# In-projection of the first mixer: more unused products, an earlier turn, a longer list of loads; in the heads, the later tile of a pair first

## The chip, the cores and the metric

The kernel runs on one core of one Trainium2 chip. The metric is device time in microseconds, the median of the runs shown. A core has TensorE (PE in the profile; its weight loads are PEld), VectorE (DVE), ScalarE (ACT), GpSimd (POOL) and SyncE (SP), whose queue issues nearly all DMAs here. The engines run on their own and meet through semaphores.

## The reference, cut to what matters

One inference step of a two-layer diffusion backbone, for 128 context tokens and 128 latent tokens, which the kernel handles side by side as 256 columns:

```
mod = silu(cond) @ w_ada[l] + b_ada[l]            # six vectors a layer: shift, scale, gate, twice
h = rmsnorm(x, g_norm_mix[l]) * (1 + sc1) + sh1
# layer 0: proj = h @ w_in; 8 MLA heads + 8 GQA heads; out projection
# layer 1: differential attention, 8 heads
x = x + gt1 * mixer(h)
h = rmsnorm(x, g_norm_ffn[l]) * (1 + sc2) + sh2
x = x + gt2 * conv_ffn(h)                          # gated, width-3 convolution over positions
```

All the data are fp32. D_MODEL is 2048, D_FF 5632. The weights are read once: 609 MB.

## The kernel before, in words

**Split products.** A weight tile `raw` (one megabyte, three buffers) is split by ScalarE into a rounded part `wh` and by VectorE into the rest `wl` (`split`, lines 257 to 259); the activations are split in the same way. One product of a 128x128 block is then three fast matmuls of 256 columns: wh by high, wh by low, wl by high (`gemm`, line 366). A plain fp32 matmul, as the unused ones are, takes two passes on TensorE.

**The modulation vectors.** `mod` is needed before the layer can be modulated, so units of w_ada (4 megabytes each, four tiles t = 0 to 3) are computed beside the products, in three ways. `HalfUnit` does half a unit for the very first rows. `sum_rows` multiplies a tile by the condition on TensorE (four matmuls of two passes a tile, which use a quarter of the array's columns each), over the four tiles of a unit into one bank; then ScalarE copies the sums to `am`, TensorE turns them (4 transposes), and VectorE reduces them into `mod` (`ada_finish`, whose steps are `copy` and `turn`). `Deep` does units on VectorE, in two halves of the rows, after a Silu of the condition's half (`silu`, line 527), in the wide tile `condb`.

**The in-projection (`mixer_ab`).** It has 23 output chunks of 128 rows and is swept in parts over the 16 blocks of input rows (a block, or row for short, is 128 of the 2048 features): `whole` takes rows 0 and 1, `halves` 2 and 3, then come three quarters of four rows each with the weights `rest`. A chunk takes 6 matmuls in the first two parts and 12 in the quarters. The results of a part are copied to or added to `proj`, `kvb` and `qb` (L1182, L1184). `part` does for each chunk: `lead` (split weights ahead until n + 8 blocks are ready; only in the first four parts), the product, the copy or add, then what `between` hangs on that chunk. In a quarter, `quarter(q)` hangs on the chunks the sums of two units in pairs of tiles, the turn of each unit, and after the second turn the four modulated rows for the next quarter (`rows`, `modulate`; ScalarE L691 and L692, VectorE L688 and L674). A tile of `rest` holds 16 blocks, the last of a quarter 12; a chunk uses 4.

**What sets the order.** `keep_order` pins instructions to program order on their engine; up to the end of the second quarter TensorE is wholly pinned (`pe.in_turn`), as are the splits of `lead`, the rows and the loads of `Feed`. What isn't pinned is placed by the framework's planner from its own estimate of when operands are ready. `Feed` holds a written list of loads, each with a home (a buffer); a load is issued in that order once its home is free, and `use` frees a home at the point of the program where its last reader stands. Of `rest`'s 18 tiles 13 are in the list; the other five are loaded by `take` when their chunk comes up. In the third quarter (`finish`) nothing of this is pinned; attention's preparations are started there chunk by chunk, `caches()` has loaded the cached keys and split the cached latent `ckc` into `kv_in`, and `Deep` begins.

**The start.** `WARM` unused products of zeros (am, 128x512, fp32) run while the first loads are on their way. Then come the sums of the first half units, the mean square of x, the first two rows, and the projection at 25.41 us.

**The heads.** For each pair of heads there are the query products (`qn`, `qr`), the keys (`kn`, copied by ScalarE at L1355), the values, scores and softmax. `pump` after a product advances the attention's chains, `Deep`, and by `row_step` the units of `ROWS`: tiles 0 and 1 are loaded as a pair (two `araw` buffers), `sum_pair` sums them 8 quarter steps later, then come 2 and 3. The sums are pinned among themselves; between them the planner may place other products.

Of the kernel before, what the change touches and what calls it, by code (L numbers as in the profile page):

```python
# [18 lines left out]
P = 128  # L19
D = 2048  # L20
KD = D // P
T = 128
# [27 lines left out]
    _n += _w  # L50
NCONST = _n
NEARLY = _AT["bada"][0] + 2 * KD
WARM = 9
RATE = {"in0": 0.35, "in": 0.5, "in3": 0.25, "heads": 0.72, "out0": 0.62, "c": 0.36, "outc": 0.36}
FRATE = {"up": 0.7, "down": 1.42}
PEW = {"heads": 1.0, "out0": 1.0, "c": 1.0}
# [38 lines left out]
def step_kernel(ctx: ExitStack, tc: tile.TileContext, A: dict):  # L95
    nc = tc.nc
    dve, act, pool, sp = nc.vector, nc.scalar, nc.gpsimd, nc.sync
    kept = []

    def keep_order(i):  # L100
        if not any(i is j for j in kept):
            kept[:] = [i]
            tc.keep_in_program_order(i)
# [16 lines left out]
    pe = TensorE()  # L120
# [20 lines left out]
    def T_(pl, shape, tag, dt=F32, bufs=None):  # L141
        kw = {} if bufs is None else {"bufs": bufs}
        return pl.tile(shape, dt, tag=tag, name=nm(tag), **kw)
# [44 lines left out]
    def start(g):  # L188
        if next(g, chains) is not chains:
            chains.append(g)  # L190
# [66 lines left out]
    def split(out_hi, out_lo, src, pin=lambda i: i):  # L257
        pin(act.copy(out_hi, src))  # L258
        pin(dve.tensor_tensor(out=out_lo, in0=src, in1=out_hi.bitcast(F32), op=ALU.subtract))  # L259
# [231 lines left out]
            feat["i"] += 1  # L491
            feat["t"] = 0

    def sum_rows(t, raw, ps=None):
        if t == 0:
            ada["ps"] = ps or T_(ppool["ada"], [P, 512], "ada", bufs=1)
        for g in range(4):
            i = pe.matmul(ada["ps"][32 * g:32 * g + 32, :], condw[:, 4 * t + g, :], raw[:, g],
                          start=(t == 0), stop=(t == 3), skip_group_check=True)
            if pinned[0]:  # L500
                keep_order(i)


    class Deep:

        def __init__(self):
            self.steps, self.due, self.rate = [], 0.0, 0.0
            self.loads, self.got, self.mid, self.ahead = [], [], False, False

        def begin(self, home, units, tiles, part, junk):  # L510
            self.home, self.tiles, self.part, self.junk, self.rate = home, tiles, part, junk, 0.0
# [14 lines left out]

        def silu(self):
            keep_order(act.activation(self.row, self.row, AF.Silu))

        def sums(self, half, i, u, t, c):  # L530
            if c == 0:
# [68 lines left out]
    def row_step(until=len(ROWS)):  # L600
        if later:
            later.pop(0)()
        if ada["i"] >= until:
            return
        l, j, q = ROWS[ada["i"]]
        t, g = divmod(ada["t"], 4)

        def load(t):
            ada["raw"] = T_(wpool, [P, 4, 512], "araw", bufs=2)
            sp.dma_start(out=ada["raw"], in_=A["w_ada"][l, j, q, t])  # L610
            return ada["raw"]

        def sum_pair(t, pair):
            for i in range(2):
                sum_rows(t + i, pair[i])

        if pinned[0]:
            if (t, g) == (2, 0):
                sum_pair(0, ada["pair"])
            if t % 2 == 0 and g < 2:  # L620
                ada["pair"] = [load(t)] if g == 0 else ada["pair"] + [load(t + 1)]
            if (t, g) == (3, 3):
                last = ada["pair"]
                later.append(lambda: sum_pair(2, last))
        else:
            if g == 0:
                load(t)
            if g == 3:
                sum_rows(t, ada["raw"])
        ada["t"] += 1  # L630
        if ada["t"] == 16:
            later.extend(ada_finish(l, j, q))
            ada["i"] += 1
            ada["t"] = 0
# [318 lines left out]
    def mixer_ab(hx, beside):  # L953
        l = 0
        with tc.tile_pool(name="ab", bufs=1) as ab:
            with tc.tile_pool(name="abp", bufs=1) as pj:
# [6 lines left out]

                def caches():
                    keep_order(sp.dma_start(out=ckc, in_=A["cache_ckv"]))
                    split(kv_in[:, :, 0, T:2 * T], kv_in[:, :, 1, T:2 * T], ckc)
                    keep_order(sp.dma_start(out=kr[:, T:2 * T], in_=A["cache_krope"]))
                    keep_order(sp.dma_start(out=kg[:, :, T:2 * T], in_=A["cache_gqa_k"]))
                    keep_order(sp.dma_start(out=vg[:, 1], in_=A["cache_gqa_v"]))
# [35 lines left out]
                def half_sums(unit):  # L1005
                    pair_sums(("half", unit.j, unit.h), unit.sums)
# [10 lines left out]
                def weights(w, parts=1):  # L1017
                    feed.add("raw", lambda: w.begin(parts))
# [20 lines left out]
                for q in (1, 2):  # L1039
                    for u, t in ((2 * q + 2, 0), (2 * q + 2, 2), (2 * q + 3, 0), (2 * q + 3, 2)):  # L1040
                        weights(rest)
                        units(u, t)
                        if (q, u, t) == (1, 4, 2):
                            feed.add("late", late_constants)
                    weights(rest)
                    weights(rest)
                feed.go()

                pe.in_turn = True
# [20 lines left out]
                nts = scaled_rows(rb0, 0, 2)  # L1070
                unit = HalfUnit(0, 0, att_bank, att_bank)
                half_sums(unit)

                def first_rows():
                    unit.copy()
                    unit.turn()
                    for c in range(2):
                        begin_row(hx, nts[c], c)

# [71 lines left out]
                    yield  # L1151

                def finish(c):
                    if c == 7:
                        deep.silu()
                        deep.rate = SIDE["in3"]
                    if c < 6:
                        start(queries(c))
                    elif c < 10:
                        start(latents(c - 6))  # L1160
                    elif c == 10:
                        start(key_rope())
                    elif c < 13:
                        start(keys(c - 11))
                    elif c == 14:
                        start(values(0))
                    elif c == 15:
                        start(values(1))
# [22 lines left out]
                def normed(q):  # L1191
                    second["nt"] = []
                    for c in range(4 * q, 4 * q + 4):
                        h = T_(tmp, [P, NT], "nt", bufs=4)
                        keep_order(dve.tensor_tensor(out=h, in0=x[:, c], in1=rb0, op=ALU.mult))
                        second["nt"].append(h)
# [20 lines left out]
                def pair(u, t):  # L1217
                    unit_pair(ROWS[u], t)
                    if t == 2:
                        second["finish"] = ada_finish(*ROWS[u])  # L1220
                        second["finish"].pop(0)()

                def turned(q=0):
                    second["finish"].pop(0)()
                    if q:
                        rows(q)
# [14 lines left out]
                def quarter(q):  # L1241
                    u = 2 * q + 2
                    return {3: lambda: pair(u, 0), 6: lambda: pair(u, 2), 8: turned, 11: lambda: pair(u + 1, 0),
                            12: lambda: normed(q + 1), 14: lambda: pair(u + 1, 2), 16: lambda: turned(q + 1)}

                def at(steps):
                    return lambda c: steps[c]() if c in steps else None
# [15 lines left out]
            with tc.tile_pool(name="abh", bufs=1) as hp:  # L1263
# [61 lines left out]
                weigh_lambda()  # L1325
                accs[:] = [0, 1]
                start(gqa_query(0))
                deep.tiles.append((ab, "kvb"))
                deep.junk = o[:, 6:8]
                deep.rate, deep.ahead = SIDE["heads"], True  # L1330
                for h in range(0, 8, 2):
                    for i in range(2):
                        ps = gemm(WQ.chunk(), qh, qlo)
                        qn[h + i] = T_(hp, [P, NT], "qn", bufs=4)
                        act.copy(qn[h + i], ps)
                        pump(RATE["heads"])
                    ps = gemm(WQ.chunk(), qh, qlo)
                    if h == 6:
                        deep.junk = ql[:, 0:2]
                    ev = T_(tmp, [P, NT], "nt", bufs=4)  # L1340
                    act.copy(ev, ps)
                    qr = T_(hp, [P, NT], "qr", bufs=2)
                    act.copy(qr[:, 0:T], ev[:, 0:T])
                    rope(qr[:, None, T:], ev[:, None, T:], 1, 32, "rcm", "rsm")
                    pump(RATE["heads"])
                    if h == 6:
                        deep.settle()
                    kn = []
                    for i in range(2):
                        if h + i < 7:  # L1350
                            start(gqa_query(h + i + 1))
                        start(gqa(h + i))
                        ps = gemm(WK.chunk(), kh, klo, 3 * T)
                        kn.append(T_(hp, [P, 3 * T], "kn", bufs=2))
                        act.copy(kn[i], ps)  # L1355
                        pump(RATE["heads"])
                    mla_pair(h, qr, kn, values())
                flush()
# [478 lines left out]
```

## Time and profile before

| | |
|---|---|
| median of 3 runs | 2295.28 us (2294.23 to 2295.8) |
| profiled execution | 2295.23 us, span 2293.4 us |
| TensorE busy | 2272.2 us, 99% |
| VectorE, ScalarE, GpSimd busy | 1880.7, 1215.1, 190.9 us |
| mean granted clock of TensorE | 0.996 |
| loads of w_in_ab, 18 of 1 MB | 9.0 us to landing (median) |
| loads of w_ada by TensorE's tile araw, 132 of 1 MB | 6.2 us to landing (median) |

A row of the timeline reads: start, length, engine, line, operation, tiles written and read, shapes, count, and in brackets the idle time of the engine before it with what ended it. A matmul's end is modelled, so busy TensorE is not TensorE at its peak; the spacing of starts says more. The granted clock is the share of full speed that TensorE's clock gate passed.

### The profile page before, as it was taken

The numbers are of one execution on the slowest core, as the hardware profiler recorded it, in microseconds if no ns is written. First come the engines' busy times: TensorE is split into PE (matmuls) and PEld (weight loads), VectorE is DVE, ScalarE is ACT, GpSimd is POOL, SyncE is SP. The second block draws the span as 40 slices with busy tenths as digits, with TensorE's granted clock in tenths as the row PEclk, the third lists the DMA queues.
The fourth block names the chain that finished last, engine by engine and source line by source line (L and its number), as shares of the span: only waits on it lengthen the run. The fifth ranks groups of instructions, "written<-read, shape, count | busy, mean of one in ns | idle before, by whom it ended". The sixth has DMA issues, their size and how long they took to land.

```text
span 2293.4 us, 47509 instructions
## 1 busy us (share of the span) xinstructions
PE 2272.2 (99%) x19496; PEld 2180.4 (95%) x19496; DVE 1880.7 (82%) x2963; ACT 1215.1 (53%) x2049; POOL 190.9 (8%) x219
## 2 busy tenths in 40 slices
PE   9999999999999999999999999999999999999998
PEld 6788888999999999999999999999999999999998
DVE  4768878889989999999978988898899955666654
ACT  4446666765553355555575454557555434555543
POOL 0011104400000000001130000023000000000011
PEclk9999999999999999999999999999999999999999
DMA  9888988777778777777778888776677655555553
GB/s 394 363 354 307 333 329 349 288 264 255 260 259 296 293 274 258 257 268 257 286 292 301 324 316 308 264 273 224 255 260 258 256 201 196 191 198 189 200 188 127
DMA packets 100121, 617.14 MB, mean 269 GB/s; under 512 B 10752, under 2 KB 18880, under 8 KB 33344
## 3 DMA queue, kind: packets, MB, share of 16 engines
q1 hardware_dynamic: 99904, 614.11, 72.4%
q8 instruction: 153, 2.51, 0.4%
q14 instruction: 64, 0.52, 0.1%
HBM read 609.32 MB, written 4.75 MB: 268 GB/s over the span
## 4 chain that ended last, share of the span: by engine, by line
PE 96%; DVE 1%; DMA 1%; ACT 1%; POOL 1%; issue 0%; SPq 0%; DVEq 0%; ACTq 0%
PE acc L110 89%; PE ada L110 3%; PE att L110 2%; DMA raw<-w_in_ab 1%; PE misc L110 0%; DVE wl L259 0%; DMA araw<-w_ada 0%; PE att L113 0%; POOL dev L837 0%; PE ada L113 0%; PE misc L113 0%; ACT wh L258 0%; DVE x L1694 0%; POOL hxc L841 0%; DVE qb L1184 0%
## 5 line engine op out<-in xcount | busy, mean ns | idle before, releaser
L110 PE MATMUL acc<-hx,wh 128*128 128x256 f32 (+1 forms) x7232 | 1248.5, 278 | 3.7 <-ACT wh L258 1.5
L258 ACT CAST wh<-raw 128x1024 fp32r<-128x1024 f32 (+1 forms) x866 | 798.6, 938 | 825.5 <-PE acc L110 697.2
L259 DVE TENSOR_TENSOR wl<-raw,wh 128x1024 fp32r<-128x1024 f32 (+1 forms) x866 | 930.3, 1091 | 245.6 <-ACT wh L258 237.9
L110 PEld LDWEIGHTS acc<-hx,wh 128*128 128x128 f32 x7232 | 1092.8, 188 | 24.7 <-issue 14.2
L110 PE MATMUL acc<-hx,wl 128*128 128x256 f32 (+1 forms) x3616 | 1001.5, 277 | 0.8 <-DVE wl L259 0.7
L110 PEld LDWEIGHTS acc<-hx,wl 128*128 128x128 f32 x3616 | 680.0, 188 | 4.3 <-issue 1.7
L110 PE MATMUL acc<-g,wh 128*128 128x256 f32 x2816 | 478.8, 276 | 0.0
L110 PEld LDWEIGHTS acc<-g,wh 128*128 128x128 f32 x2816 | 423.9, 188 | 0.0
L110 PE MATMUL acc<-g,wl 128*128 128x256 f32 x1408 | 388.0, 276 | 0.0
L483 DVE CUSTOM_DVE_ANT_0 junk<-araw,condb 128x2048 f32<-128x2048 f32 x128 | 294.1, 2297 | 0.0
L110 PEld LDWEIGHTS acc<-g,wl 128*128 128x128 f32 x1408 | 264.2, 188 | 0.0
L211 POOL TENSOR_TENSOR sqacc<-sqacc,sq 128x256 f32<-128x256 f32 x62 | 72.2, 1165 | 1442.3 <-ACT sq L207 1437.6
L110 PE MATMUL acc<-hxc,wh 128*128 128x256 f32 (+1 forms) x1056 | 189.1, 281 | 0.0
L110 PEld LDWEIGHTS acc<-hxc,wh 128*128 128x128 f32 x1056 | 161.9, 188 | 1.8 <-issue 1.7
L110 PE MATMUL acc<-hxc,wl 128*128 128x256 f32 (+1 forms) x528 | 146.8, 278 | 0.0
L110 PEld LDWEIGHTS acc<-hxc,wl 128*128 128x128 f32 x528 | 99.5, 188 | 0.2
L110 PE MATMUL acc<-wh,hxc 128*128 128x256 f32 (+1 forms) x512 | 95.0, 283 | 0.8 <-DVE nt L848 0.8
L1587 ACT ACTIVATE cv<-acc,convw 128x256 f32<-128x256 f32 x169 | 94.4, 559 | 0.0
L538 DVE CUSTOM_DVE_ANT_0 hx<-block,condb 128x1024 fp32r<-128x1024 f32 x66 | 80.4, 1218 | 4.7 <-DMA block<-w_ada 4.4
L1593 DVE SCALAR_TENSOR_TENSOR cv<-acc,convw,cv 128x254 f32<-128x254 f32 x169 | 80.8, 478 | 3.2
L110 PEld LDWEIGHTS acc<-wh,hxc 128*128 128x128 f32 x512 | 79.4, 188 | 3.7 <-issue 2.5
L1590 DVE SCALAR_TENSOR_TENSOR cv<-acc,convw,cv 128x254 f32<-128x254 f32 x169 | 80.2, 474 | 0.0
(290 smaller groups left out, 1809.3 us busy)
## 6 DMA issues: line engine op xcount, KB each, us to landing
raw<-w_up SPq DMA_DIRECT2D x176, 1024.0 KB, 4.8
araw<-w_ada SPq DMA_DIRECT2D x132, 1024.0 KB, 6.2
raw<-w_down SPq DMA_DIRECT2D x88, 1024.0 KB, 4.8
raw<-w_in_c SPq DMA_DIRECT2D x48, 1024.0 KB, 6.9
block<-w_ada SPq DMA_DIRECT2D x42, 512.0 KB, 6.5
raw<-w_in_ab SPq DMA_DIRECT2D x18, 1024.0 KB, 9.0
raw<-w_out_ab SPq DMA_DIRECT2D x16, 1024.0 KB, 7.8
raw<-w_out_c SPq DMA_DIRECT2D x16, 1024.0 KB, 5.6
```

The lines of the kernel that those rows point to most:

```text
L110: return self.placed(nc.tensor.matmul(*a, **kw))
L211: eng.tensor_tensor(out=st["acc"], in0=st["acc"], in1=sq, op=ALU.add)
L258: pin(act.copy(out_hi, src))
L259: pin(dve.tensor_tensor(out=out_lo, in0=src, in1=out_hi.bitcast(F32), op=ALU.subtract))
L483: keep_order(dve.tensor_tensor_reduce(out=T_(feat["pool"], [P, D], "junk"), in1=feat["row"][:, c], in0=feat["raw"].rearrange("p g n -> p ( ...
L538: keep_order(dve.tensor_tensor_reduce(out=self.junk, in0=self.raw, in1=self.row[:, c].rearrange("p (g n) -> p g n", g=2), scale=1.0, scala ...
L1587: pin(act.activation(y, ps, AF.Identity, scale=cw[:, 1, m:m + 1], bias=cw[:, 3, m:m + 1]))
L1590: pin(dve.scalar_tensor_tensor(out=y3[:, :, 1:], in0=p3[:, :, :T - 1], scalar=cw[:, 0, m:m + 1], in1=y3[:, :, 1:], op0=ALU.mult, op1=ALU.add))
L1593: pin(dve.scalar_tensor_tensor(out=y3[:, :, :T - 1], in0=p3[:, :, 1:], scalar=cw[:, 2, m:m + 1], in1=y3[:, :, :T - 1], op0=ALU.mult, op1=A ...
```

## The change

Seven edits, all in what runs before the first feed-forward layer's first products:

1. `WARM` goes from 9 to 15 unused products.
2. `idle_products(2)` twice: two unused fp32 products of x by x (128x512), once after the sums of the second half unit and once after its turn. They write a bank that nobody reads.
3. In the quarters, the second unit's turn and the rows of the next quarter hang on chunk 15, not 16.
4. The other five tiles of `rest` enter the list of `Feed`.
5. The split of the cached latent leaves `caches()` and hangs on chunk 3 of the third quarter.
6. `sum_pair` sums tile 1 before tile 0, and tile 3 before tile 2; start and stop flags go with that order.
7. After a Silu of `Deep` in the heads the next two copies of `kn` go to VectorE.

```
-WARM = 9
+WARM = 15
...
-    def sum_rows(t, raw, ps=None):
-        if t == 0:
-            ada["ps"] = ps or T_(ppool["ada"], [P, 512], "ada", bufs=1)
+    def sum_rows(t, raw, order=(0, 1, 2, 3)):
+        if t == order[0]:
+            ada["ps"] = T_(ppool["ada"], [P, 512], "ada", bufs=1)
         for g in range(4):
             i = pe.matmul(ada["ps"][32 * g:32 * g + 32, :], condw[:, 4 * t + g, :], raw[:, g],
-                          start=(t == 0), stop=(t == 3), skip_group_check=True)
+                          start=(t == order[0]), stop=(t == order[3]), skip_group_check=True)
...
+            self.copies = []
...
         def silu(self):
             keep_order(act.activation(self.row, self.row, AF.Silu))
+            self.copies = [dve.tensor_copy] * 2
+
+        def copy(self):
+            return self.copies.pop() if self.copies else act.copy
...
         def sum_pair(t, pair):
-            for i in range(2):
-                sum_rows(t + i, pair[i])
+            for i in (1, 0):
+                sum_rows(t + i, pair[i], (1, 0, 3, 2))
...
                 def caches():
                     keep_order(sp.dma_start(out=ckc, in_=A["cache_ckv"]))
-                    split(kv_in[:, :, 0, T:2 * T], kv_in[:, :, 1, T:2 * T], ckc)
...
                     weights(rest)
+                    weights(rest)
+                for _ in range(5):
                     weights(rest)
                 feed.go()
...
                 half_sums(unit)
+                unused = acc_bank()
+
+                def idle_products(n):
+                    for _ in range(n):
+                        pe.matmul(unused, x[:, 0, :P], x[:, 0:2].rearrange("p c n -> p (c n)"), start=True, stop=True)
+
+                idle_products(2)
 
                 def first_rows():
                     unit.copy()
                     unit.turn()
+                    idle_products(2)
...
                 def finish(c):
+                    if c == 3:
+                        split(kv_in[:, :, 0, T:2 * T], kv_in[:, :, 1, T:2 * T], ckc)
...
-                            12: lambda: normed(q + 1), 14: lambda: pair(u + 1, 2), 16: lambda: turned(q + 1)}
+                            12: lambda: normed(q + 1), 14: lambda: pair(u + 1, 2), 15: lambda: turned(q + 1)}
...
                 start(gqa_query(0))
+                deep.copies = []
...
-                        act.copy(kn[i], ps)
+                        deep.copy()(kn[i], ps)
```

## The prediction

> **What bounds the kernel now.** I read the page first, then busy time by stage, then the list of TensorE's waits, and only then the timeline of the places that the change touches.
>
> ```profile
> PE 2272.2 (99%) x19496; PEld 2180.4 (95%) x19496; DVE 1880.7 (82%) x2963; ACT 1215.1 (53%) x2049; POOL 190.9 (8%) x219
> ```
>
> ```profile
> 0.00:80.00 80.00, 74.03 (x564) 54.56 (x565) 45.02 (x116) 38.22 (x86) 1.41 (x6) 0.94 0.98 395
> 80.00:160.00 80.00, 78.07 (x656) 64.72 (x655) 51.23 (x118) 30.80 (x62) 3.34 (x4) 1.00 0.91 366
> 160.00:330.00 170.00, 168.83 (x1280) 138.57 (x1279) 140.85 (x340) 111.19 (x264) 23.28 (x27) 1.00 0.85 311
> 460.00:1155.00 695.00, 695.00 (x6133) 695.00 (x6132) 644.44 (x839) 355.95 (x494) 17.54 (x14) 1.00 0.73 269
> ```
>
> The second fence is the table of stages: length, then busy time of PE, weight load, VectorE, ScalarE, GpSimd, then granted clock, DMA share, GB/s. TensorE bounds almost all of it: 695 busy of 695 us in the first feed-forward layer. Everything edited lies before about 365 us. There PE is idle 6.0 us in the first 80, 1.9 in the next 80, 1.2 in the heads. Idle PE, a low clock and PE's own instructions are all that can be won there, a few microseconds in all; what the edits can add is of the same size.
>
> ```profile
> PE acc L110 <- ACT wh L258: 1.5, 3, 0.8
> PE acc L110 <- ACT kn L1355: 0.8, 1, 0.8
> PE acc L110 <- DVE wl L259: 0.7, 2, 0.3
> ```
>
> This is the list of PE's waits from 80 to 460 us (total, times, longest): split weights (wh, wl) that come late, and one late copy of kn. The change aims at these.
>
> **Start: six more products on zeros, four more on x.**
>
> ```profile
> 1.44 9.81 PE L110 MATMUL acc<-am 128*128 128x512 f32 x18 [1.44 <-DVE am L1651]
> ...
> 13.39 1.07 PE L110 MATMUL ada<-araw,condw 128*32 128x256 f32 x16 [2.14 <-DMA araw<-w_ada]
> ...
> 22.17 1.06 PE L110 MATMUL att<-kv_in,condw 128*32 128x256 f32 x16
> 23.79 0.44 PE L113 MATMUL att<-cst,am 128*128 128x128 f32 x2 [0.56 <-ACT am L413]
> 25.41 0.97 PE L110 MATMUL acc<-hx,wh 128*128 128x256 f32 x2 [1.19 <-ACT hx L715]
> ```
>
> ```profile
> 9.80 0.19 PEld L110 LDWEIGHTS acc<-am 128*128 128x128 f32 x1 [0.24 <-issue]
> ```
>
> ```profile
> 15.40:22.20 6.80, 6.80 (x51) 4.26 (x54) 1.69 (x8) 0.54 (x2) 0.70 (x1) 0.50 1.02 420
> 22.30:25.60 3.30, 1.55 (x23) 0.64 (x15) 1.94 (x8) 1.66 (x6) 0.00 (x0) 1.00 1.02 419
> 25.70:29.00 3.30, 3.30 (x16) 3.20 (x16) 2.53 (x6) 2.43 (x6) 0.00 (x0) 0.50 1.00 418
> ```
>
> Nine products are 18 passes, 0.43 us each at full clock (a weight load of 0.19 and 0.24 to the next), so 0.86 a product. Six more take 5.2 us: the stream ends at 16.4, not 11.25, and the first useful sums wait until then, 3.0 us later than 13.39, though their tile is there. In return the clock, which was at 0.50 from 15.4 to 22.2, may stay full: of the 9.8 us between 13.39 and 23.2 some 6.8 ran at half rate, so at full rate they need 6.4, and the sums end at 22.8; with one stretch of 3.4 us still at half, at 24.5. Before it was 23.2. Then two unused products (1.7), the turn (0.44), two more (1.7): the projection starts 3.85 us on, at 26.7 to 28.4, at full clock. Before it started at 25.41 but ran at 0.50 until 29.0, as good as a full-rate start at 27.2. So PE stands between 0.5 us ahead and 1.2 behind.
>
> Sentences on the notes: the Trainium skill (TensorE: Matmul & The Clock Gate, Part 1: The HAM clock gate) says that the gate closes after a whole idle window of about 3.4 us, and its practical advice is only to avoid idle gaps above some 3 us. By that rule gaps as short as those before 25.41 would close nothing, the new products there would be pure cost, and this term would come out about 1.5 us dearer, the whole at 2297.2. The trace differs: after gaps of 0.56 and 1.19 us in a stretch busy 1.55 of 3.30 us the clock stood at 0.50, so the measurement decides and the rule gets no chance of its own here.
>
> Whether a lead counts is decided at 66 us.
>
> ```profile
> 66.50 1.14 ACT L258 CAST wh<-raw 128x512 fp32r<-128x512 f32 x2 [6.66 <-DMA raw<-w_in_ab]
> 67.55 0.58 ACT L447 COPY am<-ada 128x512 f32<-128x512 f32 x1
> ```
>
> ```profile
> 66.14 1.04 PE L110 MATMUL ada<-kv_in,condw 128*32 128x512 f32 x8
> ...
> 68.18 0.66 PE L113 MATMUL ada<-cst,am 128*128 128x128 f32 x4
> ```
>
> DMA is busy 0.98 of the first 80 us; ScalarE idles 6.66 us for a weight tile that lands just before 66.5, splits it, and only then copies am, which the turn at 68.18 needs. A PE that is ahead waits there; one that is late has some 0.35 us of slack (its sums end at 67.2, the copy starts at 67.55). The bounds are -0.3 and +0.9; as the two ends of the start are about as likely, I take **+0.2**.
>
> **Turn at chunk 15 instead of 16, in two quarters.** ScalarE's order is written out: lead() before a chunk, then the product, then what is hung on the chunk.
>
> ```profile
> 105.29 1.14 ACT L258 CAST wh<-raw 128x512 fp32r<-128x512 f32 x2
> 108.60 0.49 ACT L691 ACTIVATE nt<-nt,mod,scl 128x128 f32<-128x128 f32 x1 [2.16 <-DVE mod L457]
> ...
> 111.95 3.74 ACT L258 CAST wh<-raw 128x512 fp32r<-128x512 f32 x7
> ```
>
> ```profile
> 107.83 0.48 PE L110 MATMUL acc<-hx,wh 128*128 128x256 f32 x2
> ...
> 112.61 0.51 PE L110 MATMUL acc<-hx,wh 128*128 128x256 f32 x2 [0.43 <-ACT wh L258]
> 113.46 0.38 PE L110 MATMUL acc<-hx,wl 128*128 128x256 f32 x1 [0.34 <-DVE wl L259]
> ```
>
> lead() splits half a tile (8 blocks, two chunks) whenever fewer than 12 blocks are ready, which in the quarters is before each even chunk. Now the split at 105.29 (lead of chunk 16) stands ahead of the four rows (108.60 to 111.95); after the turn PE has chunks 17, 18 and 19 in hand (36 products, 107.83 to about 112.0, 1.4 us a chunk), and chunk 20 finds wh at 112.61 and wl at 113.46. The rows show 0.43 and 0.34 us idle; from start to start it is 1.1 us, as a product's modelled end reaches past the next one's start. Turned at 15, the rows come ahead of chunk 16's lead. PE then has only chunks 16 and 17 in hand (8 blocks), 2.8 us, while the first split still comes 4.78 us after the turn (112.61 less 107.83). The wait moves to chunk 18 and is 2.0 + 0.5 = 2.5 us: 1.4 more. What is queued behind: chunk 18's half tile and all later splits; PE waits for them, and nothing after catches up.
>
> ```profile
> 152.22 0.60 ACT L258 CAST kv_in<-ckc 128x512 fp32r<-128x512 f32 x1
> ```
>
> ```profile
> 155.37 0.50 PE L110 MATMUL acc<-hx,wh 128*128 128x256 f32 x2 [0.82 <-ACT wh L258]
> 156.21 0.39 PE L110 MATMUL acc<-hx,wl 128*128 128x256 f32 x1 [0.34 <-DVE wl L259]
> ```
>
> In the next quarter the same wait (0.82 and 0.34 idle) lost 1.5 us, 0.4 of it by the cache's split in the middle of the rows, which the change takes away; there 2.5 less 1.5 is 1.0 more. Together **+2.4**; the bounds are -2.6 (both waits gone) and +2.8.
>
> **Weights in the list, cache split at chunk 3.**
>
> ```profile
> 150.34 7.37 SPq L284 DMA_DIRECT2D raw<-w_in_ab  x2
> ```
>
> ```profile
> DMA to landing us min/median/max: 4.8/7.2/11.1
> ```
>
> ```profile
> 164.75 2.00 ACT L258 CAST wh<-raw 128x1024 fp32r<-128x1024 f32 x2
> ```
>
> The five tiles were already issued the moment a buffer came free (150.34, then 157.4), so listing them brings nothing forward. But SP's order is now fixed: the first two stand ahead of the caches' loads, so those and condb, with no wait of their own, queue behind the tile that waits until 157.4, some 17 us later than now. With the 4.8 to 7.2 us that loads of the mixer take (the second fence, from the view of tile araw in the heads) they land at 163 to 165; the split is hung on chunk 3, just ahead of the casts of 164.75 that chunk 4 needs, and the Silu on chunk 7. So the cache's split (0.60 on ScalarE) moves to where PE already waits for casts, the last 0.2 us of the 1.5 in the list. Bounds: -0.3 (the casts come earlier) and +0.6 (the split goes ahead of them); with no row to choose by, about the middle: **+0.2**.
>
> **Heads, later tile first.**
>
> ```profile
> 174.07 1.00 PE ada L110 x8
> ...
> 209.60 1.85 PE ada L110 x16
> ...
> 359.98 0.99 PE ada L110 x8
> ```
>
> In the chain a pair in one piece takes 1.85 us; of fourteen pairs from 174.07 to 359.98 eleven are taken in two pieces, nearly all of 1.00 and 0.99, with other products between them. If that is because the second tile lands later, then with that tile first the other is always there too and the pair goes as one: 0.14 each, at most 1.6 in all. I take **-1.5**.
>
> **Two copies of kn on VectorE after the Silu.**
>
> ```profile
> 306.21 1.92 ACT L528 ACTIVATE condb<-condb 128x2048 f32<-128x2048 f32 x1
> ...
> 310.69 0.47 ACT L1355 COPY kn<-acc 128x384 f32<-128x384 f32 x1
> ```
>
> ```profile
> 311.21 0.38 PE L110 MATMUL acc<-wh,kv_in 128*128 128x256 f32 x1 [0.77 <-ACT kn L1355]
> ```
>
> The copy stands behind the Silu on ScalarE, and PE wants its bank. On VectorE, busy 140.85 of 170 us, it costs about what the 0.47 us row says and can go two microseconds sooner. Bounds -0.9 and +0.3 (what it delays on VectorE); **-0.8**, as the wait has no other late party.
>
> **Sum.** +0.2 + 2.4 + 0.2 - 1.5 - 0.8 = +0.5. The profiled execution took 2295.23 us, 0.05 under the median of 2295.28: 2295.7 predicted. Its own range, start and cache split at their ends, is 2294.7 to 2296.8. What this kernel's measurement can tell from no change is about 0.2%, 4.6 us.
>
> **Rivals.** (a) The turn does what it is for: the rows are out of the way when the weights are needed, and the waits of 1.1 and 1.5 us go. For it: the rows start 1.4 us sooner. Against: the count of blocks. -2.6 in place of +2.4: 2290.7, on the edge of 4.6 us. Chance 0.20, half of it below the edge. (b) The heads get slower. Both loads of the next pair now go out after both sums, where the first could go earlier; the second lands behind it by one megabyte, 2.5 us at 418 GB/s.
>
> ```profile
> 219.82 5.69 SPq L610 DMA_DIRECT2D araw<-w_ada  x2
> ```
>
> A load that went out at 219.82, 5.4 us before its fellow, now goes with it. Fourteen pairs come from 174.07 to 359.98, some 14 us apart; 7.2 + 2.5 and the sums' 1.85 fit, 11.1 + 2.5 + 1.85 is 1.4 us too long, and the sums are pinned, so PE may stand. It decides once these waits exceed 2.6 us (the sum without the heads' gain is +2.0), two loads at the longest; with three it is +4.2 for -1.5: 2301.4. Chance 0.05. (c) The pairs stay in two pieces, the order having been set by something else: 2297.2, chance 0.15. (d) The early lead is kept, the landing at 66.43 not binding, and the full clock's 1.7 us arrives: 2293.8, chance 0.10. The forecast has 0.50.
>
> So faster by over 0.2%: 0.10 (half of a); slower: 0.05 (b); the rest, 0.85, within. From 2291.0 to 2298.5 the range leaves out (b) and a little over half of (a).
>
> **What would show it.** Clock 1.00 from 22 to 29 us and the turn near 68.2 to 69; PE waiting about 2.5 us for wh and wl near 111 and 153, two chunks after the turn, with rows ahead of the split on ScalarE; ckc issued after 157; pairs of sixteen at 1.85 us in the heads; kn copies on VectorE and no wait near 311. The prediction is wrong if chunk 18 finds its weights split, if a new wait for araw appears, or if the order that the planner gives the heads shifts by more than these terms.

## The result, and the profile after

The changed kernel takes 2301.45 us (median of 9 runs, 2298.88 to 2303.55) against 2295.28 us in 9 runs of the kernel before: a ratio of 1.0024, 95% interval 1.0015 to 1.0033. It is about 6 us slower; 2295.7 us was forecast, with 2298.5 as the upper end. The profiled execution took 2301.87 us.

The page, and then the table of stages (columns as in the prediction; the row from 160 to 330 us stands against 168.83 us of busy TensorE at a clock of 1.00):

```profile
span 2300.1 us, 47571 instructions
PE 2277.2 (99%) x19516; PEld 2184.6 (95%) x19516; DVE 1882.9 (82%) x2974; ACT 1213.9 (53%) x2056; POOL 191.1 (8%) x219
```

```profile
0.00:80.00 80.00, 77.91 (x581) 54.83 (x582) 44.63 (x115) 38.14 (x86) 1.41 (x6) 1.00 0.97 394
80.00:160.00 80.00, 75.77 (x621) 62.12 (x621) 48.10 (x111) 29.42 (x59) 2.93 (x4) 0.98 0.84 338
160.00:330.00 170.00, 166.25 (x1269) 140.85 (x1268) 140.97 (x347) 107.84 (x261) 23.92 (x27) 0.98 0.80 303
```

TensorE has less idle time in the first 80 us, as the unused products fill it, and more in the two stages behind, where the granted clock also falls below 1. TensorE's waits from 80 to 460 us, as totals, counts and longest:

```profile
PE acc L110 <- ACT wh L258: 3.8, 3, 1.7
PE misc L110 <- DVE rv L219: 1.5, 1, 1.5
PE acc L110 <- DVE wl L259: 1.2, 4, 0.4
PE misc L110 <- POOL rr L222: 0.9, 1, 0.9
PE att L110 <- POOL rr L222: 0.8, 1, 0.8
PE att L113 <- DVE kvb L1200: 0.8, 1, 0.8
```

The wait for `kn` is gone. The waits for wh have more than doubled. Three are new, for rv, kvb and the rr that `misc` needs; they belong to the chains of keys and values ahead of the heads. The other wait for rr stands ahead of the feed-forward layer, where the kernel before has one of 0.5 us for sq.

**Start.** The timeline of TensorE:

```profile
21.63 1.07 PE L110 MATMUL att<-ql,condw 128*32 128x256 f32 x16
...
26.89 0.78 PE L110 MATMUL acc<-hx,wh 128*128 128x256 f32 x2
```

The projection starts at 26.89 us at full clock (25.41 at half before). At the end of `halves` TensorE is 0.3 us behind (75.18 us against 74.88 for the first product of the first quarter).

**The turn.** Timelines of TensorE in both quarters, and of ScalarE in the second:

```profile
111.49 0.50 PE L110 MATMUL acc<-hx,wh 128*128 128x256 f32 x2 [1.73 <-ACT wh L258]
112.33 0.39 PE L110 MATMUL acc<-hx,wl 128*128 128x256 f32 x1 [0.34 <-DVE wl L259]
155.22 0.50 PE L110 MATMUL acc<-hx,wh 128*128 128x256 f32 x2 [1.72 <-ACT wh L258]
156.05 0.43 PE L110 MATMUL acc<-hx,wl 128*128 128x256 f32 x1 [0.33 <-DVE wl L259]
```

```profile
151.22 0.50 ACT L696 ACTIVATE nt<-nt,mod,scl 128x128 f32<-128x128 f32 x1 [1.78 <-DVE mod L457]
...
154.24 0.40 ACT L697 CAST hx<-nt 128x256 fp32r<-128x256 f32 x1
154.55 3.74 ACT L258 CAST wh<-raw 128x512 fp32r<-128x512 f32 x7
```

The rows stand ahead of the split, and chunk 18 waits 1.7 and 0.3 us idle (2.4 from start to start) in both quarters. What was not forecast follows it: the clock.

```profile
108.50:111.90 3.40, 1.67 (x14) 1.36 (x12) 2.75 (x7) 3.31 (x9) 1.47 (x2) 1.00 0.00 0
152.80:156.20 3.40, 1.35 (x10) 0.95 (x9) 2.74 (x7) 3.34 (x9) 1.46 (x2) 1.00 0.56 236
156.30:159.70 3.40, 3.40 (x18) 3.40 (x18) 1.93 (x4) 1.99 (x4) 0.00 (x0) 0.50 0.53 181
193.80:197.20 3.40, 1.12 (x6) 0.72 (x6) 3.40 (x14) 1.36 (x4) 0.96 (x1) 1.00 0.66 221
197.20:204.00 6.80, 6.10 (x28) 4.74 (x32) 6.51 (x18) 2.58 (x6) 0.64 (x1) 0.50 0.39 120
```

In the second quarter the wait leaves TensorE busy for 1.35 us of a 3.4 us window, and the next 3.4 us run at 0.50: 1.6 us lost on top (spacing of starts against that of the same products at full clock). The same wait in the first quarter left 1.67 us busy, and nothing followed.

**Before the heads.** The last two rows of that fence are a second stand (a stretch in which TensorE mostly waits) that nobody foresaw. TensorE and ScalarE in the third quarter:

```profile
194.40 0.44 PE L113 MATMUL att<-cst,kvb 128*128 128x128 f32 x2 [0.76 <-DVE kvb L1200]
196.31 0.68 PE L110 MATMUL misc<-cst,rr 128*128 128x128 f32 x4 [1.47 <-DVE rv L219]
197.90 1.22 PE L110 MATMUL misc<-cst,rr 128*128 128x128 f32 x4 [0.91 <-POOL rr L222]
```

```profile
188.37 1.12 ACT L258 CAST wh<-raw 128x512 fp32r<-128x512 f32 x2
...
197.73 0.30 ACT L1152 COPY kg<-kvb 128x128 f32<-128x128 f32 x1 [0.99 <-DVE kvb L1150]
197.93 2.17 ACT L258 CAST wh<-raw 128x512 fp32r<-128x512 f32 x4
```

TensorE walks through the keys' chain link by link, because chunk 16's weights are split only at 197.93 us, behind the copy of `kg`. VectorE shows what is in that stretch:

```profile
192.58 1.22 DVE L543 CUSTOM_DVE_ANT_0 hx<-block,condb 128x1024 fp32r<-128x1024 f32 x1
...
196.08 1.22 DVE L543 CUSTOM_DVE_ANT_0 hx<-block,condb 128x1024 fp32r<-128x1024 f32 x1
...
198.87 0.68 DVE L259 TENSOR_TENSOR wl<-raw,wh 128x512 fp32r<-128x512 f32 x1
```

Two sums of `Deep` stand between the earlier splits and this one. Their block landed at 191.62 us, as SP issued it at 182.55 behind the last listed tile (157.76 before). Waits of 4.5 us (0.9 before) and 3.0 us at half clock are lost here.

**Heads.** In the chain of what ended last, every pair is one piece now (16 matmuls of 1.85 us, or 2.61 at half clock):

```profile
202.53 2.61 PE ada L110 x16
217.97 1.85 PE ada L110 x16
...
405.95 1.85 PE ada L110 x16
```

**The sum over the span.** Each start of a TensorE instruction to the next, less the usual spacing of its kind, gives after less before: +8.6 us of unused products, -4.9 of half clock and -4.5 of waits at the start, +2.2 of waits at the two turns and +1.6 of half clock behind them, +3.6 of waits and +3.0 of half clock before the heads, -3.5 at the edges of the modulation's sums (in the third quarter and the heads), -0.9 for kn, and +1.5 in what remains: +6.7 us of span. Of what remains 1.1 us belong to the start, where TensorE is 0.3 us behind though its three terms come to -0.8.

### The profile page after: what moved, and what is told of

It is laid out like the page before. It is cut to its first block, busy times and chain, and to the rows that moved or that the text cites. A ratio compares the mean times of both kernels' runs of the same rounds, so it can differ in the third digit from the quotient of the medians.

```text
span 2300.1 us, 47571 instructions
## 1 busy us (share of the span) xinstructions
PE 2277.2 (99%) x19516; PEld 2184.6 (95%) x19516; DVE 1882.9 (82%) x2974; ACT 1213.9 (53%) x2056; POOL 191.1 (8%) x219
## 4 chain that ended last, share of the span: by engine, by line
PE 96%; DVE 1%; DMA 1%; issue 1%; ACT 1%; POOL 0%; DVEq 0%; SPq 0%; POOLq 0%; ACTq 0%
PE acc L110 89%; PE ada L110 3%; PE att L110 2%; DMA kv_in<-w_ada 1%; DMA araw<-w_ada 0%; PE misc L110 0%; DVE wl L259 0%; PE ada L113 0%; PE att L113 0%; PE misc L113 0%; DMA ckc<-cache_ckv 0%; ACT wh L258 0%; DVE x L1711 0%; POOL rr L222 0%; DVE ql L543 0%
```

## The experiments

Edits are numbered as in the list of the change. All ran beside the kernel before (2295.17 to 2295.51 us). This table, worked out from the spacing of starts and the timelines, is what the sections below rest on: lost time as waits + half clock, in the two turns, in the third quarter, and from the heads to the first feed-forward layer; and when `Deep`'s 33rd sum starts, the first after its second Silu.

| kernel | median us | turns | third quarter | heads and on | 33rd sum |
|---|---|---|---|---|---|
| before | 2295.28 | 2.6 + 0 | 0.9 + 0 | 1.5 + 0 | 308.2 |
| after | 2301.45 | 4.8 + 1.6 | 4.5 + 3.0 | 1.5 + 0 | 316.2 |
| e1_turn16 | 2296.67 | 2.2 + 0 | 3.9 + 2.5 | 1.5 + 0 | 311.8 |
| e2_nolist | 2308.11 | 5.4 + 1.6 | 0.3 + 0 | 11.7 + 2.5 | 321.9 |
| e3_turn_alone | 2304.92 | 5.4 + 1.5 | 0.3 + 0 | 6.7 + 1.6 | 319.5 |
| e4_list_alone | 2304.81 | 2.2 + 0 | 3.9 + 2.6 | 5.0 + 1.5 | 323.7 |
| e5_heads | 2294.81 | 2.6 + 0 | 0.8 + 0 | 2.5 + 0 | 308.0 |
| e6_start | 2297.2 | 2.6 + 0 | 1.4 + 0 | 2.4 + 0 | 306.7 |
| e7_lead_first | 2296.85 | 2.4 + 0 | 3.8 + 2.7 | 1.2 + 0 | 311.8 |
| e8_start_heads | 2296.19 | 2.6 + 0 | 1.4 + 0 | 5.0 + 0 | 306.3 |
| e9_list_nolead | 2303.99 | 4.8 + 1.6 | 0 + 0 | 7.1 + 2.1 | 323.7 |
| e10_lead_first_nolead | 2304.64 | 2.3 + 0 | 0 + 0 | 11.6 + 2.4 | 317.2 |
| e11_best | 2296.24 | 2.7 + 0 | 0.9 + 0 | 4.0 + 0 | 305.6 |
| e12_heads_junk | 2292.74 | 2.6 + 0 | 1.3 + 0 | 1.2 + 0 | 308.6 |
| e13_all_mended | 2304.68 | 2.3 + 0 | 0 + 0 | 11.8 + 1.9 | 318.8 |
| e14_junk_alone | 2295.34 | 2.6 + 0 | 1.3 + 0 | 1.5 + 0 | 309.2 |
| e15_mended_no_start | 2302.76 | 2.3 + 0 | 0 + 0 | 8.2 + 3.0 | 316.1 |
| e16_mended_no_list | 2291.95 | 2.7 + 0 | 1.4 + 0 | 1.2 + 0 | 308.1 |
| e17_mended_light | 2295.26 | 2.4 + 0 | 0 + 0 | 3.4 + 1.5 | 292.7 |
| e18_no_list_light | 2296.69 | 2.8 + 0 | 0.9 + 0 | 3.4 + 0 | 291.6 |

### Which part costs it: turn or list

The changed kernel with the turn back at 16, and with 13 tiles in the list; and the kernel before with the turn alone, and with list and cache split alone (edits 4 and 5).

```
e1_turn16, on after:      -  15: lambda: turned(q + 1)}     +  16: lambda: turned(q + 1)}
e2_nolist, on after:      -  weights(rest)                  (the last one per quarter and the loop of five)
e3_turn_alone, on before: -  16: lambda: turned(q + 1)}     +  15: lambda: turned(q + 1)}
e4_list_alone, on before: edits 4 and 5 as in the diff of the change
```

> The changed kernel with the second unit's turn back on chunk 16. Theory T (the turn): with the rows ahead of chunk 16's split the weights come 2.4 us late in each quarter, the clock falls for 3.4 us after the second wait, the tile loaded into that split's buffer goes out 6.3 us late, and from that come the late weights and the 3.6 us of standing at the end of the third quarter. So nearly all of the 6.2 us goes: 2294 to 2296.5, tile 14 issued near 150.5 us, PE waiting 1.1 us at chunk 20. Theory L (the list): the five listed tiles, pinned ahead of the caches' loads, make the third quarter late by themselves. So only the waits of the two quarters and the first low clock go, about 4 us less: 2297 to 2299, the standing before the heads and the second stretch of low clock stay.

> The changed kernel with 13 tiles of rest in the list again; the turn stays on chunk 15, the cache's split on chunk 3. Theory T: the buffers still come free 6 us late, so the third quarter is as late as in the changed kernel: 2300 to 2302.5. Theory L: the caches are loaded near 141 us again, the standing near 193 us and the second low clock go: 2296 to 2298.5.

> The kernel before with the turn on chunk 15 and nothing else. Theory T: PE waits 2.4 to 2.9 us at chunk 18 of both quarters, +2.7 us together, +1.7 for 3.4 us at half clock, and the third quarter late on top: 2299 to 2303. Theory L: only the waits and the low clock: 2298 to 2300, no standing before the heads.

> The kernel before with all 18 tiles in the list and the cache's split on chunk 3, nothing else. Theory T: the tiles are issued when their buffers come free, as before: 2294.5 to 2296.5. Theory L: the caches and the Silu's operand are loaded behind the pinned tiles, the third quarter stands: 2297.5 to 2301.

Ratios to before: e1 1.0005 (0.9996 to 1.0014), e2 1.0058 (1.0046 to 1.0071), e3 1.0042 (1.0029 to 1.0054), e4 1.0041 (1.0029 to 1.0054). Each part alone costs 9 us, both together with the other edits cost 6, and taking the list out of the change makes it 7 us slower. So the parts do not add, and both theories missed: e2, e3 and e4 came out above either range, e1 between the two. The table does separate where each acts: the longer wait and the half clock behind it come with the turn, the stand in the third quarter with the list (three of three kernels with it, none without). What neither theory had is the last stage. TensorE's waits from 80 to 460 us in e2:

```profile
PE acc L110 <- ACT hx L258: 10.6, 1, 10.6
PE acc L110 <- ACT wh L258: 3.8, 2, 2.1
```

and ScalarE's timeline in e3, where the same wait is 5.8 us:

```profile
349.10 0.37 ACT L258 CAST hx<-att 128x256 fp32r<-128x256 f32 x1 [11.42 <-DVE mod L538]
```

ScalarE stands 11.4 us before it rounds the last heads' output into hx. It waits for `Deep`, which throws the unneeded product of its sums into `o[:, 6:8]`, the very chunks that the last heads write, and which the last projection's order (`PAIR_LATE`) leaves to the end. In the kernel before `Deep`'s last sum there starts at 338.4 us and the cast ends in time; in e2 it starts at 351.4.

### The edits of start and heads, and the mended turn

```
e5_heads, on before:       edits 6 and 7
e6_start, on before:       edits 1 and 2
e8_start_heads, on before: edits 1, 2, 6 and 7
e7_lead_first, on after:   -  15: lambda: turned(q + 1)}
                           +  15: lambda: (lead(rest, 12), turned(q + 1))}
```

> The kernel before with only the two edits in the heads (the later tile of a pair summed first; the copies of kn on VectorE). Theory S (the parts add up by stretch): the changed kernel spends 5.8 us less in the heads than the kernel before for what these two edits touch, so 2289.5 us (2288.5 to 2291), all pairs in the heads' sums, no wait for kn, and no stand at the start of the last projection. Theory D (the end of the heads decides): the unpinned instructions are placed anew, Deep's last sum with its output in hx comes later than about 340 us, and TensorE waits 3 to 10 us for ScalarE's hx near 342 to 350 us: 2293 to 2300 us.

> The kernel before with only the edits at the start (one more unused product at half clock and the others in their new number). Theory S: the start alone, +0.3 us as measured at every landmark from 57 to 106 us of the changed kernel: 2295.6 us (2294.8 to 2296.4), full clock from 6 us on. Theory D: the same at the start, and whatever the end of the heads makes of a 0.3 us shift: nothing, if Deep's last sum into hx keeps its place.

> The changed kernel, with the half tile that chunk 16's product needs split ahead of the turn's rows rather than behind the product of chunk 15. Theory T (the turn's cost is the wait for that half tile and what follows from it): the waits of 2.4 us in the second quarter and 3.0 us in the third go, with them the half clock near 156 us, tile 14 is issued near 150.5 instead of 156.6 us; the stand before the heads (list) stays: 2295 us (2293.5 to 2297). Theory L (the list is the whole loss of the third quarter, the turn's wait only moves): the wait is found again one product later, and the time stays at 2299 to 2302 us.

> The kernel before with the edits at the start and in the heads, without the turn, the list and the caches' move. Theory S: the sum of those two, 2289.9 us (2288.8 to 2291.5). Theory D: a stand of 3 to 10 us near 342 to 350 us at the start of the last projection, 2293 to 2300 us.

Ratios: e5 0.9999 (0.999 to 1.0008), e6 1.0009 (0.9999 to 1.0018), e8 1.0005 (0.9996 to 1.0013), e7 1.0007 (0.9998 to 1.0016).

e7 settles the turn: splitting the half tile ahead of the rows takes the waits at the turns from 4.8 to 2.4 us, and the half clock near 156 us and 4.6 us of time go with it. The stand before the heads stays. Theory T held.

Theory S did not. It took the 5.8 us by which the changed kernel seemed to pass the heads faster for the worth of these edits; e5 gains 2.4 us at the pairs' edges and loses some of it again at 341 us, for a net 1.6 us of span in its profile and no gain beyond the interval. ScalarE's timeline in e5 shows where:

```profile
333.55 0.59 ACT L447 COPY am<-ada 128x512 f32<-128x512 f32 x1 [1.94 <-PE ada L110]
338.63 0.37 ACT L258 CAST hx<-att 128x256 fp32r<-128x256 f32 x1 [4.49 <-DVE mod L543]
338.90 0.38 ACT L258 CAST hx<-acc 128x256 fp32r<-128x256 f32 x1
340.99 1.05 ACT L258 CAST wh<-raw 128x1024 fp32r<-128x1024 f32 x1 [1.71 <-PE acc L110]
```

TensorE reaches the last projection 6 us sooner than before, and ScalarE still has to wait until 338.6 us for the same sum of `Deep`; weights queue behind. Whoever gains time in the heads runs into this. e6, at 2297.2 us, came out above its range (2294.8 to 2296.4).

### The stand before the heads, and the junk

`lead` splits ahead where tiles are in hand. The text ahead of the prediction says that it acts only in the first four parts and that nothing of the kind is pinned in the third quarter. That was misread: `finish` is handed to `part` as `between`, so `lead` is called there too, and in the kernel before finds no begun tile. With five more tiles in the list it finds them, and pins their splits.

```
e9_list_nolead, on after:
-                        if between:
+                        if between and k0 < 12:
                             lead(W, n + 8)
e10_lead_first_nolead, on after: the edits of e7 and e9
e12_heads_junk, on before: edits 6 and 7, and
+                    if h == 4:
+                        deep.junk = qb[:, 0:4].rearrange("p (a b) n -> p a (b n)", a=2)
e11_best, on before: edits 1, 2, 6 and 7, the turn of e7, the junk of e12
```

> The changed kernel, with lead() left out of the third quarter (the list itself stays). Theory P (pinned splits): with tiles of the list in hand, lead() acts in the third quarter too, where before it found none, so that the weights' splits are held in program order there; those of chunk 16 stand on VectorE behind Deep's first two sums (192.6 and 196.1 us), and the first of these needs a block that lands at 191.6 us. Without it the stand of some 3.5 us and the half clock of 3.0 us before the heads go: 2294.9 us (2293 to 2297), the casts there are again of 1024 columns (1.05 us). Theory R (SP's order): the caches', condb's and the block's loads, queued behind the listed tiles, cause the stand by themselves: it stays, 2300 to 2302 us.

> The changed kernel, with the half tile split ahead of the turn's rows (as in the run with the lead first, 2296.85 us) and lead() left out of the third quarter. Theory P: 2296.85 less the 3.4 us of waits and 2.7 us of half clock that it still has there, 2290.7 us (2289.5 to 2293), unless Deep, which starts 8 us later than in the kernel before, is late at the end of the heads: then up to 3 us of it come back as a wait near 340 us. Theory R: 2296 to 2297.5 us.

> The kernel before with the edits of the start and of the heads, the turn at chunk 15 with the half tile split ahead of its rows, no list, and Deep's junk in the dead queries from the fifth head on instead of in hx. Theory D (the end of the heads holds the gain back: ScalarE's casts into hx wait for Deep's last sums with their junk there): the 2.2 us of waits near 343 us of the run with start and heads go, and 0.3 us at the turns: 2293.7 us (2292 to 2295). Without D: 2295.5 to 2297 us.

> The kernel before with only the edits in the heads, and Deep's junk in the dead queries from the fifth head on instead of in hx. Theory D: ScalarE no longer idles 4.5 us for Deep's sum ahead of its last casts into hx (338.6 us in the run with the heads' edits alone), the weights for the last projection are split in time, and the 1.66 us of waits at 341 to 343 us go: 2293.1 us (2292 to 2294.3). Without D: 2294.5 to 2295.5 us, the waits stay.

In e9 and e10 the stand is gone: no wait at all in the third quarter, the casts of 1024 columns again (1.04 to 1.06 us). The list's tiles are still there, so pinning by `lead` made the stand, and theory P is right on its mechanism. Which pinned neighbour held the split (`Deep`'s sums, or ScalarE's copy of kg) is read from one trace and was not tried apart. The times are wrong: 2303.99 us (ratio 1.004, 1.0026 to 1.0053) and 2304.64 (1.0038, 1.0025 to 1.0051). In e10 TensorE reaches the last projection 4.7 us ahead of the kernel before, and then

```profile
PE acc L110 <- ACT hx L258: 10.4, 1, 10.4
```

e12 moves the junk out of hx: ScalarE's wait goes, and the heads' edits now gain: 2292.74 us, 0.9988 (0.9979 to 0.9997). e11 gains nothing (2296.24, 1.0004, 0.9995 to 1.0013); it has the start's edits and the mended turn in addition, and waits of 1.1 us for kn and 1.4 us for a sum's tile that e12 has not.

### Is it the junk, or Deep's lateness?

```
e13_all_mended, on after: the edits of e7, e9 and the junk of e12
e15_mended_no_start:      e13 without edits 1 and 2
e14_junk_alone, on before: the junk of e12
e16_mended_no_list, on before: edits 6 and 7, the turn of e7, the junk of e12
e17_mended_light: e13, e18_no_list_light: e16, each with
+            if self.light and t % 2:
+                self.got.append(self.last)      # in Deep.load, in the heads only
+                return
```

> All edits of the change, mended in three places: the half tile split ahead of the turn's rows, no lead() in the third quarter, Deep's junk in the dead queries from the fifth head on. Against the run with the first two of these (2304.64 us, 11.6 us of waits and 2.4 us of half clock at the end of the heads). Theory D (the junk in hx is the whole of it): those 14 us go but for about 1 us of other waits there: 2291.5 us (2289.5 to 2293.5). Theory E (Deep's late sums cost the time by any path: VectorE and the loads have no room for them): the wait is found again for wl or a sum's tile between 340 and 370 us, 2296 to 2302 us.

> The kernel before with only Deep's junk moved. Theory D: before has no wait at the end of the heads (the last sum into hx ends at 339.6 us, just hidden), so nothing is won: 2295.4 us (2294.4 to 2296.4). If the moved junk were worth something by itself (VectorE's and ScalarE's order), the 2.8 us that the heads' edits with moved junk gained would be partly its own: 2293 to 2294.4 us.

> As the mended kernel, but with the start of the kernel before. Theory D: the start's edits cost 0.3 to 0.8 us at the landmarks from 57 us on, so this is that much faster than the mended kernel with them: 2290.9 us (2289 to 2293). Theory E: 2295 to 2302 us.

> The heads' edits, the turn at chunk 15 with the half tile first, and Deep's junk moved; start and list as before. Against the heads' edits with moved junk alone (2292.74 us): the turns' waits are 1.17 and 1.54 us instead of 1.11 and 1.48, so nothing is won by the turn: 2292.8 us (2291.8 to 2293.8). If the list is worth what the run without lead() in the third quarter showed there (its third quarter took 41.5 us instead of 43.3), the mended kernel with the list and the old start is 1 to 2 us faster than this one.

> The mended kernel (2304.68 us), with every second load of Deep's tiles in the heads left out: each tile is summed twice, so Deep's numbers are not the reference's, while its sums on VectorE keep their count. Theory E (Deep's late loads and sums cost the time by any path): Deep's 33rd sum comes near 306 us instead of 318.8, the 10.8 us of waits and 1.9 us of half clock at the start of the first feed-forward layer go, 2291 us (2289 to 2294). If Deep is not the cause: 2302 to 2305 us.

> The kernel with the heads' edits, the turn with the half tile first and the junk moved (2291.95 us), with every second load of Deep's tiles in the heads left out as in the other run. It has no wait for Deep, so theory E expects next to nothing: 2291.5 us (2290 to 2293). If less traffic gains by itself, 2 us or more less.

e13 takes 2304.68 us (1.0039, 1.0025 to 1.0052), e15 2302.76 (1.0033, 1.002 to 1.0045): the junk was not the whole of it. Both lie above the range of theory E too. e13 is 3.0 us ahead of the kernel before at the first product of the feed-forward layer, and stands there:

```profile
429.30 0.71 PE L110 MATMUL att<-cst,rr 128*128 128x128 f32 x4 [0.70 <-POOL rr L222]
436.96 0.58 PE L110 MATMUL acc<-u,wh 128*128 128x258 f32 x1 [6.96 <-ACT u L757]
439.92 0.58 PE L110 MATMUL acc<-u,wh 128*128 128x258 f32 x1 [2.37 <-DVE u L758]
```

VectorE has just done `Deep`'s last sums:

```profile
432.94 1.35 DVE L543 CUSTOM_DVE_ANT_0 u<-block,condb 128x1024 fp32r<-128x1024 f32 x1
...
434.57 0.15 DVE L564 TENSOR_TENSOR mod<-mod 128x8 f32<-128x8 f32 x1
```

So `Deep`, once late, is paid for at the next place that needs it, first hx, then u. e14 (2295.34, 0.9999, 0.999 to 1.0008) shows that moving the junk alone wins nothing. e17, with half of `Deep`'s loads in the heads left out, has its 33rd sum at 292.7 us and takes 2295.26 us (0.9999, 0.9989 to 1.0008): the stand at the feed-forward layer is gone and 9.4 us with it. It stays 4 us above its expectation, as the earlier sums crowd the heads (two waits of 2.8 us together near 295 us, and 1.5 us of half clock). The control e18 shows that crowding without the list (2.3 us of waits; 2296.69 us, 1.0008, 0.9999 to 1.0018): it is 4.7 us slower than e16, not equal to it as expected, so lighter loads gain nothing by themselves. In the table every kernel with the list, or with the turn as changed, has its 33rd sum at 311.8 us or later, every other one at 309.2 or sooner (e17 and e18 apart). Why it comes late is open: its loads share SP's queue and the planner's order with everything else, and no run took these apart. The traces do show where: in e10, e13 and e15 the third sum starts at 203.9 to 205.6 us (204.4 before), the 32nd at 302.6 to 305.7 us (293.6 before), so there the delay arises in the heads.

e16 is the fastest: 2291.95 us (2291.04 to 2294.04), 0.9986 (0.9977 to 0.9994), faster than both kernels. It has the heads' edits, the junk moved, and the turn with the half tile first; the last of these is worth nothing that can be told from e12.

## Why the prediction was wrong, by its own steps

- **Start, +0.2.** Within its bounds (-0.3 to +0.9), but at the upper end: clock 1.00 throughout, as stated, and the first quarter's first product, which ends `halves`, at 75.4 us in the mean of eleven kernels with these edits (74.6 to 75.8), at 74.6 in nine without (74.0 to 75.2). That is 0.75 us, of which the changed kernel's own profile shows 0.3. Over the whole time the edits cost more. Four pairs of kernels differ by them alone, and all four are slower with them: e6 than before by 1.9 us, e8 than e5 by 1.4, e13 than e15 by 1.9, e11 than e16 by 4.3, the last clear of the intervals. So the term holds for the start itself; from the heads on e11 has 2.8 us more of waits than e16, and why they come with these edits is open.
- **Turn, +2.4.** The mechanism was right, place and size of the wait included (chunk 18; 2.4 us in both quarters, the difference to before being 2.2). Missing was what a wait does afterwards: 1.6 us at half clock, and tiles released later (the first listed extra tile was issued at 156.63 instead of 150.34 us). e7 puts the whole at 4.6 us, about twice the term; with that one repair the time, 2296.85 us, lies inside the forecast's range. The prediction had a row in hand that would have told it (busy 1.55 of 3.30 us, then 0.50) and used it for the start alone.
- **List and cache split, +0.2.** The failed step: the term that is furthest off. The prediction followed SP's order rightly (ckc issued at 161.90 us, after 157 as it said, though it landed at 167.10, not at 163 to 165) and costed the cache split, but took the splits of the third quarter for unpinned whatever the list holds. Pinned by `lead`, they cost 3.6 us of waits and 3.0 us of half clock in the changed kernel, 6.6 us where the term had 0.2; alone, list and cache split cost 9.3 us (e4), by the table 5.6 before the heads and 5.0 from there on, less 1 us elsewhere. Taking the pinning away removes the stand, but e9 (2303.99 us) shows no gain of time from it: there TensorE waits for the late `Deep` instead.
- **Heads, -1.5.** Right in its mechanism: all pairs in one piece, 2.1 us less at the edges of the nine that came in two in the heads, 0.23 each where 0.14 was reckoned; 3.5 with the pairs of the third quarter. Rivals (b) and (c) did not come in the changed kernel, nor did (d): TensorE has no lead. Waits for a sum's tile, as (b) has them, do stand in e8 (1.9 us) and e11 (1.4 us).
- **kn on VectorE, -0.8.** The wait of 0.93 us went, but not by the stated way. The two copies on VectorE run at 284 and 287 us, 30 us ahead of the Silu (314.25 us) behind which they were to help: the Silu comes ahead of them in the program but waits for its load, which lands at 312.99 us. In e8 and e11 the same wait is back (0.9 and 1.0 us).
- **The sum.** Even with the right terms a sum over stages does not hold here: time won ahead of `Deep`'s deadline is lost again when `Deep` is late (e9, e10, e13). The changed kernel escapes this, as far as its trace shows, because its TensorE is late too: ScalarE waits 4.9 us for `Deep` there as well, until 346.68 us, and nobody waits for ScalarE. The prediction named such a shift in the heads among what would make it wrong, and gave it no price or chance.

Rival (a), the turn that works, needed the half tile first, and even then (e7) the waits are as before.

## What to carry to other kernels

Follow a background chain (here the sums on VectorE) to the place where its results, or even its scrap output, are next needed: a deadline that is just hidden gives no line in the list of waits, and it decides what gains and losses ahead of it are worth. Before listing or pinning one kind of instruction, look for every helper that acts on what is in hand, as it may begin to pin others. And price a wait of 2 us with the half clock that may follow it.

## What the runs showed of the hardware

The runs show how little idleness is followed by half clock on TensorE, and that the same idleness need not be. The granted clock changes on a grid of 3.41 us: in the changed kernel 156.25 and 197.21 us are 12 steps apart. At the turns, where only in-projection products run, a window with 1.15 to 1.53 us of busy TensorE was followed by one at 0.50 in four cases of five, and one with 1.67 us or more never. The table of stretches in e9, the first quarter's turn and the second's:

```profile
108.90:112.30 3.40, 1.53 (x12) 1.13 (x10) 2.75 (x7) 3.31 (x9) 1.47 (x2) 1.00 0.00 0
112.30:115.70 3.40, 3.21 (x15) 3.21 (x16) 2.36 (x5) 2.43 (x5) 0.00 (x0) 0.50 0.46 152
153.30:156.70 3.40, 1.68 (x15) 1.48 (x15) 2.50 (x7) 3.31 (x9) 1.35 (x2) 1.00 0.82 345
156.80:160.20 3.40, 3.06 (x26) 2.86 (x26) 2.71 (x5) 2.93 (x7) 0.02 (x1) 1.00 0.28 77
```

The wait is the same 2.4 us in both, but it lies otherwise on the grid: one window is left with 1.53 us of busy TensorE, the other with 1.68, and the half clock behind it costs 1.6 us or nothing. In e9 the first turn paid, in the changed kernel the second. The bound is not sharp: in e2 a window of 1.52 us had no such sequel, and before the heads, with small products in between, 1.7 to 2.0 us of modelled busy time had one (e1, e4, e7). The Trainium skill (TensorE: Matmul & The Clock Gate, Part 1: The HAM clock gate) says that the window is free-running and 3413 ns long; the grid agrees. It also says that the clock falls after a whole idle window; here windows that were busy for 1.1 to 1.5 us sufficed, and the measurement decides.
